# Moving four additions of a Strassen attention kernel from VectorE to accumulating DMAs issued by GpSimd

## The chip, the cores and the metric

The kernel runs on one core of one Trainium2 chip. The metric is the device time of one execution in microseconds (us). Two runs of the kernel before took 783.65 and 784.54 us, median 784.1.

The engines are named as in the profile: PE is TensorE's matmuls and PEld its weight loads, DVE is VectorE, ACT is ScalarE, POOL is GpSimd, SP is SyncE (it issues DMAs here). SBUF is the core's working memory; PSUM, in eight banks, is where matmuls leave their results.

## The reference

Plain attention over 8 batches, 2048 positions and a width of 512, in float32:

```python
scores = np.matmul(q, k.transpose(0, 2, 1)) / np.sqrt(d_k)
attn_weights = special.softmax(scores, axis=-1).astype(np.float32)
return np.matmul(attn_weights, v)
```

## The kernel before

The kernel works in float16 with float32 sums and cuts matmuls by Strassen's scheme in Winograd's form: a product of two-by-two blocks takes seven block products and some additions, in place of eight products. It does so for the scores (L271 to L326, class Group), for the weights times v (class Pair, from L474), and once more, a level deeper, for three of the seven products of that second stage (class Leaf). Softmax is computed without a maximum: ScalarE takes the exponential of the scores, and a column of ones beside v gives the row sums.

The work is cut in 32 periods, four to a batch; a period g covers 256 queries, in two blocks of 128, called a and b. Each period has an order written out by hand (SEQUENCES), a string of words; the periods 2 to 29 use four orders in turn, by the remainder of g by 4, and the first two and the last two have their own. Every engine and queue executes its instructions in the order in which the words put them, so the order of the words is the order of PE, DVE, ACT, POOL and SP, each for itself. A prime behind a word means that it belongs to the period before. The words that matter here:

- a dot: the next of 28 products of the scores of a period, two matmuls of 512 columns each (L299). L309 to L325 evacuate them: ScalarE copies, VectorE adds from PSUM (L319, L322), ScalarE takes exponentials (L239); e is one more exponential.
- a1, a5, a6, a7 and the same with b: a block's four products of the outer level, eight matmuls of 256 columns each (L512). Behind each stands a ScalarE copy of the result to the block's float32 rows in SBUF (L521, L524, L527, L530). Rows are cut in four quarters of 256 columns: o2l, o1l, o1r, o2r. Product 5 goes to o2r, 6 to o1r, 7 to o2l, 1 to o1l.
- f and h, with a or b: the additions that the change touches (add_right). f does o1r = o1r + o2r, once products 5 and 6 have been copied; h does o2r = o2r + o2l, once product 7 has been copied. Since h writes what f reads, h comes after f.
- L1 to L7: the products of the leaf level, twelve matmuls of 128 columns each (L424), for both blocks at once: L1, L2, L6 and L3 give parts of block a, L5, L7 and L4 of block b. Each is followed by a VectorE addition to the rows (L431), which therefore has to find f and h done. They share one PSUM bank (L5 and L3 a second), so that a leaf product also waits for the addition of the one before.
- s0 to s3, xa0 to xb3, K, q, V, u, w, n: sums of weights, k, q and v on VectorE, f16 to f16.
- S0, S1: the scaled rows of a block (ScalarE, L444), and their stores, issued by SP (L447).
- lq, lk, lv: a load of a quarter of the next batch's q, k or v, 512 KB in f16, with a cast from float32, issued by POOL (L131, L211). tq, tk: its transpose by a DMA that SP issues (L155). q and k go through two staging buffers, so a load waits, on POOL, for the transpose that frees its buffer.

Of the kernel before, what the change touches and what calls it, by code (L numbers as in the profile page):

```python
# [12 lines left out]
def kernel(  # L13
# [21 lines left out]
    nc = tc.nc  # L35
# [24 lines left out]
    NP = B * NQT  # L60
# [117 lines left out]
    add, sub = nc.vector.tensor_add, nc.vector.tensor_sub  # L178
# [270 lines left out]
    def halves(g, m):  # L449

        o = rows[g % 2][:, m, 0:4 * H].rearrange("p (h d) -> p h d", h=4)
        return o[:, 1:3], o[:, 0:4:3]

    def out_rows(g, m, half):
        b, sp = divmod(g // 2, NSP)
        n = (2 * sp + half) * NT + g % 2 * 2 + m
        return out[b, n * P:(n + 1) * P].rearrange("p (h d) -> p h d", h=2)
# [13 lines left out]
    class Pair:  # L471
# [58 lines left out]
            nc.scalar.copy(out=self.o2l, in_=self.x[:, 0:H])  # L530

        def add_right(self, n):
            if self.leaf and n == 1:
                add(self.o1r, self.o1r, self.o2r)
            elif self.leaf:
                add(self.o2r, self.o2r, self.o2l)

        def scaled(self, out_, src, r):
            nc.scalar.activation(out=out_, in_=src, func=COPY, scale=r)
# [6 lines left out]
        def ready(self, half):  # L546

            self.parts[half] += 1
            if self.parts[half] == 2:
                nc.sync.dma_start(  # L550
                    out=out_rows(self.g, self.m, half), in_=halves(self.g, self.m)[half]
                )

# [51 lines left out]
    def pv(g, which):  # L605
# [3 lines left out]
        if (g, which[0]) not in pairs:  # L609
# [19 lines left out]
        ),  # L629
        'second': (  # L630
# [3 lines left out]
        ),  # L634
# [4 lines left out]
        ),  # L639
# [5 lines left out]
        ),  # L645
# [4 lines left out]
        ),  # L650
# [5 lines left out]
        ),  # L656
        'alone': (
            "s2' xa0' b7' xa2' xa1' fb' . L6' s4' lv1' e ya0 a1 hb' ya1 xb0 L5' . ya2 a5 xb1 L7' "
            "ya3 tk2' K20' xa3' a6 fa b5 xb2 K30' a7 xa0 q1' L4' L3' xb3 ha b1 s1 S0' L2 b6 xa2 "
            "S1' "  # L660
        ),
        'last': (
            "b1 s3' b7' xb0 xa1' L1' s2' a5 xa3' fb' s4' hb' a1 b5 L6' a3 L5' xb1 a6 L7' xb2 L3' "
            "xb3 a2 L4' S0' a7 S1' b3 b6 b2 b7 a4 b4 "
        ),
    }

# [224 lines left out]
```

## Time and profile before

One execution was profiled. All times of instructions come from it.

| | |
|---|---|
| median of two runs | 784.1 us |
| the profiled execution | 782.76 us |
| its span, first to last instruction | 780.9 us |
| PE busy | 775.5 us |
| DVE busy | 742.4 us |
| ACT busy | 630.8 us |
| POOL busy | 72.2 us |
| granted TensorE clock | 1.00 |
| HBM read, written | 100.70 MB, 33.55 MB |

A line of the profile's groups gives the line in the kernel, the engine, the operation, the tile written and those read, the shape, and the count; behind the bar the busy time of all, the mean of one in ns, and the engine's idle time in front of them. Matmuls are pipelined, so their recorded durations overlap; the step from one start to the next tells the pace. A line of the waits gives the total, the number of waits and the longest one. In the timeline a line begins with start and length.

### The profile page before, as it was taken

Reading aid. Unit: us, or ns where it says so; the run is one execution under the profiler, and the core shown is the slowest. Engines: PE = TensorE matmul, PEld = TensorE weight load, DVE = VectorE, ACT = ScalarE, POOL = GpSimd, SP = SyncE. Lnnn points to the kernel's source line nnn. Section 1 sums busy time; section 2 is a strip of 40 time slices with the busy share of each in tenths; the row PEclk is TensorE's granted clock in tenths of the full one; section 3 lists DMA queues with packets and bytes.
Section 4 is the critical chain, followed back from the end, with each engine's and each line's share of the span. In section 5 each row is a group of like instructions: output and inputs, shape, how many; then the busy total and the mean of one; then the engine's idle time right before and its main releaser. Section 6 shows DMA issues by size and latency. Waiting matters only on the chain.

```text
span 780.9 us, 17260 instructions
## 1 busy us (share of the span) xinstructions
PE 775.5 (99%) x6681; PEld 538.5 (69%) x6681; DVE 742.4 (95%) x1460; ACT 630.8 (81%) x1146; POOL 72.2 (9%) x106
## 2 busy tenths in 40 slices
PE   9999999999999999999999999999999999999997
PEld 6566766667666776667666676766766667766687
DVE  5799999999999999999999999999999999999996
ACT  5887788887888878888788887888788887888863
POOL 4011100011000110001100100001000010000000
PEclk9999999999999999999999999999999999999999
DMA  9999776889859999578895879859788797930024
GB/s 226 182 170 153 160 169 134 157 158 169 181 100 148 197 155 187 111 153 179 111 205 118 175 152 149 188 116 167 164 151 174 135 152 156 168 95 29 28 72 146
DMA packets 196386, 115.97 MB, mean 149 GB/s; under 512 B 122448, under 2 KB 187088, under 8 KB 196304
## 3 DMA queue, kind: packets, MB, share of 16 engines
q0 software_dynamic: 49664, 49.29, 43.0%
q1 hardware_dynamic: 146352, 65.26, 34.0%
q8 instruction: 52, 0.85, 0.4%
q10 hardware_dynamic: 288, 0.33, 0.1%
q14 instruction: 30, 0.25, 0.1%
HBM read 100.70 MB, written 33.55 MB: 172 GB/s over the span
## 4 chain that ended last, share of the span: by engine, by line
PE 99%; DMA 1%; SPq 0%; ACT 0%; DVE 0%; issue 0%
PE t L299 48%; PE t L512 29%; PE t L424 19%; PE t L244 1%; PE t L259 1%; PE t L165 1%; DMA rows<-in_k_dram 1%; PE t L597 0%; SPq L141 0%; ACT stage L813 0%; SPq L760 0%; DVE rows L542 0%; PE t L790 0%
## 5 line engine op out<-in xcount | busy, mean ns | idle before, releaser
L299 PE MATMUL t<-qraw,kraw 128*128 128x512 f16 x732 | 192.2, 379 | 0.0
L512 PEld LDWEIGHTS <-s 128*128 128x128 f16 x1536 | 150.1, 98 | 50.4 <-issue 0.2
L424 PEld LDWEIGHTS <-right 128*128 128x128 f16 x2232 | 140.1, 97 | 38.3
L299 PEld LDWEIGHTS <-kraw 128*128 128x128 f16 x984 | 93.1, 98 | 77.1
L299 PE MATMUL t<-qs,ks 128*128 128x512 f16 x492 | 139.9, 379 | 0.0
L512 PE MATMUL t<-vt,s 128*128 128x257 f16 (+1 forms) x1024 | 131.8, 273 | 0.0
L239 ACT ACTIVATE right<-cz 128x1024 f16<-128x1024 f32 x123 | 130.2, 1058 | 1.3 <-DVE cz L319 0.8
L431 DVE TENSOR_TENSOR rows<-t,rows 128x384 f32<-128x384 f32 x217 | 119.7, 552 | 7.9 <-PE t L424 4.4
L313 ACT COPY cz<-t 128x512 f32<-128x512 f32 x122 | 71.5, 586 | 33.9 <-PE t L299 31.7
L299 PEld LDWEIGHTS <-ks 128*128 128x128 f16 x738 | 67.5, 98 | 39.9 <-issue 0.3
L239 ACT ACTIVATE right<-t 128x512 f16<-128x512 f32 x138 | 83.2, 606 | 12.5 <-PE t L299 3.8
L319 DVE TENSOR_TENSOR cz<-t,cz 128x512 f32<-128x512 f32 x123 | 84.3, 685 | 6.0 <-PE t L299 6.0
L239 ACT ACTIVATE left<-t 128x512 f16<-128x512 f32 x128 | 76.6, 599 | 16.3 <-PE t L299 13.4
L322 DVE TENSOR_TENSOR cz<-t,cz 128x512 f32<-128x512 f32 x123 | 84.3, 685 | 3.2 <-PE t L299 2.9
L316 ACT COPY cz<-t 128x512 f32<-128x512 f32 x123 | 72.9, 592 | 13.7 <-PE t L299 11.4
L444 ACT ACTIVATE rows<-rows,scales 128x512 f32<-128x512 f32 x124 | 82.8, 722 | 0.1
L424 PE MATMUL t<-vh,right 128*128 128x128 f16 (+1 forms) x1004 | 76.4, 218 | 0.0
L309 ACT COPY t<-t 128x512 f32<-128x512 f32 x121 | 70.2, 580 | 4.8
L299 PE MATMUL t<-qs,kraw 128*128 128x512 f16 x246 | 73.2, 379 | 0.0
L299 PE MATMUL t<-qraw,ks 128*128 128x512 f16 x246 | 73.1, 379 | 0.0
L512 PE MATMUL t<-vh,left 128*128 128x256 f16 x512 | 66.7, 273 | 0.0
L512 PE MATMUL t<-vh,s 128*128 128x256 f16 x512 | 66.4, 273 | 0.0
(93 smaller groups left out, 997.3 us busy)
## 6 DMA issues: line engine op xcount, KB each, us to landing
out_dram<-rows SPq DMA_DIRECT2D x127, 256.0 KB, 2.8
vh<-in_v_dram POOLq DMA_DIRECT2D x32, 512.0 KB, 9.6
stage<-in_q_dram POOLq DMA_DIRECT2D x28, 512.0 KB, 6.0
stage<-in_k_dram POOLq DMA_DIRECT2D x28, 512.0 KB, 6.8
right<-in_k_dram POOLq DMA_DIRECT2D x2, 512.0 KB, 12.9
rows<-in_q_dram SPq DMA_DIRECT2D x2, 256.0 KB, 3.6
cz<-in_q_dram SPq DMA_DIRECT2D x2, 256.0 KB, 4.4
cz<-in_k_dram SPq DMA_DIRECT2D x2, 256.0 KB, 4.5
```

The costliest lines, as they stand in the source:

```text
L165: nc.tensor.transpose(tr[:, m, dc, :], src[:, n + m, dc * P:(dc + 1) * P], ident)
L239: nc.scalar.activation(out=out_, in_=in_, func=EXP, scale=inv_sqrt_d)
L299: nc.tensor.matmul(dst[:], lhs[:, j, dc, :], rhs[:, :, dc, :], start=(n in (1, 5) and dc == 0), stop=(dc == 1), skip_group_check=True,)
L309: self.edges[0](out=self.y[:], in_=self.x[:])
L313: self.edges[1](out=self.cz[:, 0, :], in_=self.z[:])
L316: nc.scalar.copy(out=self.cz[:, 1, :], in_=self.x[:])
L319: nc.vector.tensor_add(self.cz[:, 0, :], self.x[:], self.cz[:, 0, :])
L322: nc.vector.tensor_add(self.cz[:, 1, :], self.z[:], self.cz[:, 1, :])
L424: nc.tensor.matmul(to[:, h * Q:h * Q + w], lhs[:, j, h, :], rhs[:, j, 0:w], start=(n in (1, 2, 5) and h == 0 and j == 0), stop=(j == NK - ...
L431: nc.vector.tensor_add(o, part, o)
L444: nc.scalar.activation(out=o, in_=o, func=COPY, scale=scales[:, g % 2, m, 1 - h:2 - h])
L512: nc.tensor.matmul(dst[:, 0:width], lhs(j), rhs(j), start=(first and j == 0), stop=(j == NJ - 1), skip_group_check=True,)
```

## The change

In the periods 1 to 29 the additions f and h of both blocks are made by DMAs that POOL issues, with the DMA adding its source to what stands at its destination. Period 0 and period 30 keep VectorE's additions (period 31 has none). All orders but the first are rewritten, with the same words except for their places. One store of the last block moves from SP's queue to ACT's. The diff, with the orders of the periods 1, 30 and 31 left out:

```diff
         def add_right(self, n):
-            if self.leaf and n == 1:
-                add(self.o1r, self.o1r, self.o2r)
-            elif self.leaf:
-                add(self.o2r, self.o2r, self.o2l)
+            if not self.leaf:
+                return
+            out, more = (self.o1r, self.o2r) if n == 1 else (self.o2r, self.o2l)
+            if 0 < self.g < NP - 2:
+                nc.gpsimd.dma_start(out=out, in_=more, accum_op=mybir.AluOpType.add)
+            else:
+                add(out, out, more)
...
             if self.parts[half] == 2:
-                nc.sync.dma_start(
+                last = self.which == "b" and self.g == NP - 1
+                (nc.scalar if last else nc.sync).dma_start(
                     out=out_rows(self.g, self.m, half), in_=halves(self.g, self.m)[half]
                 )
...
         1: (
-            "b7' e . w0' fb' w1' . L2' a1 w3' hb' . a5 s3' . . e . a6 w2' xa2' . . xa3' u3' . "
-            "L1' s2' . fa L5' tq1' . . . . L6' e . s4' n3' a7 ha . xb2 . tk1 lk3 xb0 xb1 L7' . . "
-            ". . e L3' xb3 . L4' . . . lk2 b1 s1 S1' L2 q0 q2 . s3 S0' . L1 . b6 e K00 b5 "
+            "e u2' xb0 xa0' . . a1 . . e V31' w1' n0' xa1' n1' xa3' . . . n3' a5 L2' . . . s3' "
+            "tq1' . hb' L1' s2' . . e xb1 a6 fa w3' . u3' . n2' L6' w2' . . s4' tk1 a7 lk3 e . "
+            "xb2 L5' L7' xb3 . . . . L3' . K00 . q0 ha q2 . L4' lk2 S0' b1 s1 s3 S1' b5 b6 . L2 "
+            ". . e L1 "
         ),
         2: (
-            "s2' b7' tk2' K20' . . xa0' . q1' fb' e L6' K30' ya0 hb' lv1' xa1' ya1 L5' K10' a1 "
-            "xa2' . . L7' . a5 ya2 . a6 q3 . . xb0 lq2 ya3 a7 s4' . xb1 xa3' xb2 . xa0 . b1 tk3 "
-            ". L3' . b5 . e xb3 . L4' s1 . b6 fa . xa1 S0' . e ha L2 . . b7 . fb . s3 hb L5 . . "
-            "lv3 . L1 S1' . K01 . lq3 "
+            "b7' fb' s2' K20' q1' tk2' . hb' . . e lv1' K30' L6' a1 xa0' xa1' ya0 K10' ya1 . . . "
+            "q3 L5' . a5 . xa2' . lq2 . a6 ya2 fa s4' . L7' e xb0 a7 . tk3 . L3' . L4' ya3 . S1' "
+            ". ha b1 . xb1 . . S0' xa0 e b6 xa3' xb2 xb3 . . . b5 xa1 . s1 s3 . b7 K01 . xa2 xa3 "
+            "K11 lv3 . fb . . lq3 "
         ),
         3: (
-            "e K21' . . a1 K11' a5 s2' . a6 xb0 lv2 . K31' L6' . e s4' . xa2' L7' . . fa tq3' . "
-            "xa3' L3' . xb2 tq2' . a7 . e L4' S1' . xb1 . . . xb3 e ha b1 s1 L2 . . s3 xa0 b5 . "
-            ". L1 s2 xa1 S0' . b6 fb . . . s4 xa2 b7 hb . q0 q1 . . . "
+            "a5 K21' a1 . . L2' a6 e . fa K31' hb' lv2 . L1' . a7 s2' . . . b1 s4' xb0 e tq3' . "
+            "ha L6' . xb1 tq2' . xb2 . xb3 s1 L5' . . . . e e L7' L3' s3 b6 . xa0 b5 . xa1 fb . "
+            "L4' S0' . . L2 . xa2 S1' . . L1 s2 s4 q0 . b7 . . . "
         ),
         0: (
-            "e L6' . V01 . L5' . V00 L7' . . q2' a1 e q3 . . ya2 ya0 . . lq0 e L3' . lk0 u0 V10 "
-            "tq0 V11 ya1 xb0 a5 . . . xa3' n0 a6 V20 . . V21 . . S0' b5 V30 u2 a7 xa0 . u1 n1 fa "
-            ". . lq1 ya3 b1 n2 . xb1 tk0 . xb2 . V31 L4' lv0 e . b6 . . xb3 s1 ha . lk1 . S1' "
-            "xa1 "
+            "q1' q2' . . e V00 a1 . V01 L6' V10 . . hb' . q3 L5' . . . e lq0 ya0 . lk0 L7' V30 "
+            "tq0 . L3' e . L4' a5 V20 S0' . V11 ya2 . . ya1 ya3 . . a6 fa S1' V21 . xb0 xa3' xb2 "
+            ". . lq1 a7 ha b5 . tk0 b1 . xb1 xb3 u0 e . u1 b6 fb lv0 . xa2 . . s1 . lk1 . w0 b7 "
         ),
```

More of the change, by code (lines that the diff above doesn't have):

```diff
@@ L630 @@
         'second': (
[3 rows of a table removed]
-        ),
[4 rows of a table removed]
-        ),
[5 rows of a table removed]
-        ),
[4 rows of a table removed]
-        ),
[5 rows of a table removed]
[3 rows of a table added]
+        ),
[5 rows of a table added]
+        ),
[5 rows of a table added]
+        ),
[4 rows of a table added]
+        ),
[4 rows of a table added]
         ),
         'alone': (
-            "s2' xa0' b7' xa2' xa1' fb' . L6' s4' lv1' e ya0 a1 hb' ya1 xb0 L5' . ya2 a5 xb1 L7' "
-            "ya3 tk2' K20' xa3' a6 fa b5 xb2 K30' a7 xa0 q1' L4' L3' xb3 ha b1 s1 S0' L2 b6 xa2 "
-            "S1' "
+            ". b7' xa0' s2' K20' xa1' e ya0 q1' xa2' lv1' . ya1 xb0 a1 L6' fb' ya2 a5 xb1 s4' "
+            "ya3 a6 b5 xa3' K30' fa xb2 a7 hb' L5' ha b1 tk2' xa0 L7' L3' b6 xb3 S0' L4' xa1 fb "
+            "b7 xa2 S1' L2 "
         ),
         'last': (
-            "b1 s3' b7' xb0 xa1' L1' s2' a5 xa3' fb' s4' hb' a1 b5 L6' a3 L5' xb1 a6 L7' xb2 L3' "
-            "xb3 a2 L4' S0' a7 S1' b3 b6 b2 b7 a4 b4 "
+            "a5 s1' xb0 a1 s3' xa3' L1' s2' hb' b1 xb1 b5 L5' a3 L6' s4' a6 xb2 a2 L7' xb3 L3' "
+            "S0' a7 L4' b3 b6 S1' b2 b7 a4 b4 "
         ),
```

6 rows, old and new, of the table SEQUENCES are left out of this document.

## The prediction

> **What bounds the kernel now.** The page's first part says which engines are full, and its fourth which of them the end waits for.
>
> ```profile
> span 780.9 us, 17260 instructions
> PE 775.5 (99%) x6681; PEld 538.5 (69%) x6681; DVE 742.4 (95%) x1460; ACT 630.8 (81%) x1146; POOL 72.2 (9%) x106
> PE 99%; DMA 1%; SPq 0%; ACT 0%; DVE 0%; issue 0%
> ```
>
> VectorE is 95% busy and is what the change relieves, but the chain of waits goes through TensorE for 99% of the span. Two things can hide in such a 99%: TensorE may wait in short pieces, and the modelled ends of its matmuls may cover gaps. The view of waits settles the first, and the view by stretches says where idle time is at all (columns: stretch, length, then busy time and instructions of each engine, granted clock, DMA share, GB/s).
>
> ```profile
> PE t L790 <- DVE vt L747: 1.2, 1, 1.2
> PE t L165 <- ACT stage L813: 0.3, 1, 0.3
> ```
>
> ```profile
> 0.00:20.00 20.00, 18.50 (x170) 13.25 (x171) 11.12 (x25) 10.30 (x17) 9.66 (x21) 1.00 1.05 226
> 20.00:100.00 80.00, 80.00 (x623) 51.76 (x622) 74.53 (x155) 64.33 (x116) 9.10 (x13) 1.00 1.01 167
> 100.00:700.00 600.00, 600.00 (x5148) 414.42 (x5146) 583.96 (x1131) 500.61 (x912) 53.43 (x72) 1.00 0.81 155
> 700.00:760.00 60.00, 60.00 (x550) 43.57 (x549) 58.79 (x122) 46.99 (x87) 0.00 (x0) 1.00 0.10 36
> 760.00:781.00 21.00, 16.98 (x199) 15.51 (x196) 13.99 (x33) 8.54 (x18) 0.00 (x0) 1.00 0.43 151
> ```
>
> TensorE's two waits are both in the opening, which the change doesn't touch. From 20 to 760 us it is never idle, at the full granted clock. For the second question I take the step from one start to the next in the timeline, which no modelled end can blur, and the counts of the three matmul lines from 100 to 700 us (L299, L512 and L424 in this order).
>
> ```profile
> 412.52 0.59 PE L299 MATMUL t<-qs,ks 128*128 128x512 f16 x2
> 412.95 1.04 PE L512 MATMUL t<-vh,s 128*128 128x256 f16 x8
> 413.83 0.59 PE L299 MATMUL t<-qs,ks 128*128 128x512 f16 x2
> 415.56 0.83 PE L424 MATMUL t<-vu,right 128*128 128x128 f16 x12
> 416.23 1.03 PE L299 MATMUL t<-qraw,kraw 128*128 128x512 f16 x4
> ```
>
> ```profile
> 100.00:700.00 600.00, 357.75 (x1416) 1.00 0.81 155
> 100.00:700.00 600.00, 204.61 (x1608) 1.00 0.81 155
> 100.00:700.00 600.00, 146.69 (x2124) 1.00 0.81 155
> ```
>
> Two matmuls of 512 columns take 412.95 - 412.52 = 0.43 us, eight of 256 take 413.83 - 412.95 = 0.88, and twelve of 128 take 416.23 - 415.56 = 0.67. Packed at that pace the counts need 1416 x 0.2165 + 1608 x 0.1094 + 2124 x 0.0558 = 306.6 + 175.9 + 118.5 = 601 us, in a stretch of 600. So TensorE streams without gaps, and VectorE, though nearly full, is never late. That is the main fact: the change removes no matmul, so outside the two ends it has nothing to win.
>
> **The change part by part.** *The additions that go.* The rows of L534 and L536, and the timeline around one of them:
>
> ```profile
> L536 DVE TENSOR_TENSOR rows<-rows 128x256 f32<-128x256 f32 x62 | 26.0, 419 | 0.0
> L534 DVE TENSOR_TENSOR rows<-rows 128x256 f32<-128x256 f32 x62 | 25.9, 418 | 0.0
> ```
>
> ```profile
> 400.52 0.41 DVE L534 TENSOR_TENSOR rows<-rows 128x256 f32<-128x256 f32 x1
> 400.85 0.68 DVE L319 TENSOR_TENSOR cz<-t,cz 128x512 f32<-128x512 f32 x1
> ```
>
> 62 of each is two blocks in 31 periods; the periods 1 to 29 give 4 x 29 = 116 of the 124. VectorE loses 116 x 0.419 = 48.6 us of records; by the steps, 0.33 us each, 38 us of its time, or 4 x 0.33 = 1.3 us in a period of about 23.8 us. On the path this is worth zero: the cover is TensorE's unbroken stream, and it stays. A bound from above on any gain is TensorE's whole idle time, 1.50 + 4.02 us in the first and last stretch, 0.7%.
>
> *The DMAs that come.* 116 issues on POOL, each 128 partitions x 1 KB. No row shows an accumulating DMA or one from SBUF to SBUF. The nearest (KB each, then the median us from issue to landing), with POOL's own issue time:
>
> ```profile
> out_dram<-rows SPq DMA_DIRECT2D x1, 128.0 KB, 1.9
> stage<-in_q_dram POOLq DMA_DIRECT2D x28, 512.0 KB, 6.0
> stage<-in_k_dram POOLq DMA_DIRECT2D x28, 512.0 KB, 6.8
> vh<-in_v_dram POOLq DMA_DIRECT2D x32, 512.0 KB, 9.6
> kraw<-stage SPq DMA_TRANSPOSE x28, 4.3
> ```
>
> ```profile
> L131 POOL DMA_DIRECT2D stage<-in_q_dram x28: 742/742/757, 36.9 to 669.3; - x28
> DMA to landing us min/median/max: 5.5/6.4/21.8
> ```
>
> The same bytes from the same tile land 1.9 us after an SP issue. A load through POOL, of four times the bytes, takes 6.0. The price, from issue to landing, lies between 1.9 and 6.0; I take 3.0, nearer to the row of equal size, with POOL's 0.74 us of issue and some 0.4 for the second read added to it. POOL's time is 116 x 0.74 = 86 us beside its 72: no bound. By the Trainium skill (DMA: Bandwidth & Descriptors, Anatomy of one DMA — SWDGE (gpsimd) path) a DMA of this path costs about 2.0 us plus its bytes at 436 GB/s; for 128 KB I estimate 2.3 us by it, the sum below would be the same, and no row here shows such a transfer alone.
>
> *What the price is worth.* The additions of one block are in series: hx rewrites what fx reads, so POOL issues hx only when fx has landed. Whoever comes late is the first leaf addition (L431) of that block, and behind it on VectorE, in order, the sums of scores (L319, L322) whose PSUM banks TensorE needs. So I walk the new orders with the steps above: 0.43 a dot, 0.87 an a or b product, 0.67 a leaf product, and the copy that frees each addition:
>
> ```profile
> L530 ACT COPY rows<-t 128x256 f32<-128x256 f32 x62 | 23.1, 373 | 9.5 <-PE t L512 9.5
> ```
>
> The tightest place is order 2. The end of b6 lies in order 1, with ". L2 . . e L1" behind it (2.64 us); in order 2, b7' ends at 0.87 and L5' at 0.87 + 3 x 0.43 + 0.67 + 0.87 + 3 x 0.43 + 0.67 = 5.68. So from b6 to the end of L5' there are 8.32 us. fb can start 0.37 after b6, hb not before b7's copy at 2.64 + 0.87 + 0.37 = 3.88. At 3.0 us each, fb lands at 3.4 and hb at 6.9: 1.4 us to spare. VectorE begins to wait once twice the price plus 0.37 passes 8.32, at 3.97 us. The next is order 0: b7 ends 1.30 before the end of order 3, and L5' ends 4.81 into order 0, so after the copy hb has 6.11 - 0.37 = 5.74 us. The hb' that order 1 issues stands on POOL behind two loads of order 0, lv0 and lk1: lk1 waits for tk0 (word at 16.8, plus 4.3 of landing, 21.1), is issued by 21.9 and lands some 7 to 10 us later, 28.7 to 31.5; the period ends at 22.5, so hb lands by about 10 of order 1, and L5' ends there at 14.0. The a blocks have more: L2 ends 9 us or more after the copy that frees ha, with one load at most between. So at 3.0 us no leaf addition waits, and the term is zero; at 4.5 it would be 7 x 1.05 us of VectorE's waiting, which the 1.3 us freed in each period absorb.
>
> *The loads behind them on POOL.* POOL now does a queue of its own waits:
>
> ```profile
> POOL stage L131 <- DMA qraw<-stage: 250.9, 24, 20.9
> POOL stage L131 <- DMA kraw<-stage: 177.4, 22, 21.3
> ```
>
> Until now it stood waiting for a transpose and issued the load at once. In order 0, lq0 and lk0 now stand behind hb', which is issued about when the period begins; 6.0 to 6.8 us later they land, before tq0's word at 7.2. If they come late, SP stands at tq0, with the stores of S0' (10.3) and tk0 (16.8) behind it, and the first sum that needs q is q0 late in order 1, over 25 us on. Zero, and the cover is that distance.
>
> *DMA traffic.* The row of POOL's queue:
>
> ```profile
> q0 software_dynamic: 49664, 49.29, 43.0%
> ```
>
> 116 x 128 = 14848 packets more, at 43.0% / 49664 each, are 13% of the engines' span, twice that if a read-modify-write costs double. The steady stretch has a share of 0.81 and the opening ran at 1.01 to 1.05 with more GB/s, so there is room: zero.
>
> *The new orders and the last store.* The words of TensorE are the same in number, so their worth is zero while nothing waits. The last b store moves from SP's queue to ACT's, beside another store of the tail; in the last stretch that can save or cost one issue, under 0.4 us.
>
> Sum against the profiled execution: 780.9 span + 0, and 1.9 around it, 782.8. The median of the runs shown is 1.3 above that execution, so I forecast 784.1.
>
> **The rivals.** *Slow additions* (slower). If an accumulating DMA costs what a q load costs, 6.0 us, then in order 2 hb lands at 0.37 + 12.0 = 12.37 against 8.32: VectorE stands 4.05 us, in each of the 7 periods with this order, and 0.26 in the 7 of order 0. The freed 1.3 us absorbs part, so TensorE loses 2.7 to 4.3 us seven times, 19 to 30: about 808. It passes 2% (15.7 us, 2.2 a place) at a price of 5.1 to 5.8 us. For it speaks that every POOL row is at 5.5 or more; against it that those move four times the bytes, from HBM.
>
> *Behind the loads* (slower). Additions share POOL's DMA queue with loads. If a load took the longest landing of the row above, 21.8, in order 0, hb would land at 21.9 + 21.8 - 22.5 = 21.2 of order 1, 7.2 after L5' ends; seven times, 50 us: 834. That longest one is from the opening's rush, so I give it little.
>
> *Descriptors held by VectorE.* If POOL could only issue in VectorE's pauses, each DMA would be later by up to one VectorE instruction, 0.7 us in the rows above: 3.7 each, still under 3.97, and 784 to 786. Against it: 28 issues took 742 to 757 ns while VectorE was 97% busy. The Trainium skill (SBUF — State Buffer, SBUF: two separate sides) warns of this starvation, for VectorE's two-port modes; the issue times here don't show it.
>
> *VectorE sets the pace after all* (faster). Then its 38 us would come back, 746. TensorE's packed steps exclude it; only the ends, at most 5.5 us, could shrink: 778.6.
>
> **How the numbers follow.** Zero sum, a price up to about 5 us: 0.79, with its own range from 783 to 790. Slow additions: 0.15. Behind the loads: 0.03. Held descriptors: 0.02, within 2%. Faster at the ends: 0.01, and faster by over 2% is excluded but for an error of mine: 0.01 for the class. So within 2% (about what a measurement of this kernel can tell from no change) 0.81, slower 0.18. The range goes from 782.0, the ends a little shorter, to 798.0, which takes in prices up to some 5 us; what is left out above is about 0.17.
>
> **What would show it.** Right: the accumulating DMAs land in a median near 3 us; VectorE's busy time falls to about 694 us (8 additions stay); TensorE is still never idle from 20 to 760 us; waits of L431 for such a DMA are rare and under 1 us. Wrong: landings of 4 us or more, L431 or L319 waiting for rows<-rows in order 2, with TensorE idle just behind it; POOL's loads later and SP standing at a transpose while K sums on VectorE wait.

## The result and the profile after

The changed kernel takes 818.4 us (median of two runs, 816.4 and 820.4) against 784.1: a ratio of 1.045, interval 1.043 to 1.047, so 34 us slower, above the top of my range at 798.0. The profiled execution took 816.36 us around a span of 814.4. Where the runs of a kernel below spread by more than 1.5%, the text compares those within 1.5% of its fastest.

The page's parts 1 and 4 of the changed kernel, to be read beside those of before:

```profile
span 814.4 us, 17487 instructions
PE 783.9 (96%) x6681; PEld 540.2 (66%) x6681; DVE 712.9 (88%) x1344; ACT 626.7 (77%) x1146; POOL 175.0 (21%) x222
PE 71%; DMA 18%; issue 4%; DVE 3%; ACT 2%; POOL 1%; SPq 0%; POOLq 0%; DVEq 0%; ACTq 0%
```

VectorE is lighter, as meant, and now also idle: it is busy for 88% of a longer span, where it was 95%. The chain of waits, which was TensorE for 99%, goes through DMAs for 18%. The view by stretches, for the same 600 us as before:

```profile
100.00:700.00 600.00, 576.93 (x4883) 395.25 (x4882) 530.57 (x981) 469.48 (x860) 138.79 (x168) 0.99 1.05 169
```

Before, this stretch held 5148 matmuls without a pause. Now it holds 4883, and TensorE is idle for 600 - 576.93 = 23 us of it. The 265 missing matmuls are 265 / 5148 x 600 = 31 us of work: most of the 34 us. Idle time accounts for 23 of the 31; PE's busy time for the same 6681 matmuls grew by 8 us as well, from 775.5 to 783.9 (the last section has a reason for part of that). The DMA share went from 0.81 to 1.05. The groups and DMA rows (KB each, us from issue to landing) that answer to those of the prediction:

```profile
L537 POOL DMA_DIRECT2D rows<-rows x116 | 101.1, 880 | 481.5 <-ACT rows L527 169.2 <-ACT rows L530 64.6 <-DVE s L352 46.7
```

```profile
L539 DVE TENSOR_TENSOR rows<-rows 128x256 f32<-128x256 f32 x8 | 3.3, 415 | 0.0
```

```profile
rows<-rows POOLq DMA_DIRECT2D x116, 128.0 KB, 4.9
stage<-in_q_dram POOLq DMA_DIRECT2D x28, 512.0 KB, 8.9
stage<-in_k_dram POOLq DMA_DIRECT2D x28, 512.0 KB, 7.4
qraw<-stage SPq DMA_TRANSPOSE x28, 8.3
kraw<-stage SPq DMA_TRANSPOSE x28, 7.8
```

```profile
DMA to landing us min/median/max: 2.6/4.9/16.6
```

The last fence is the landing row of L537 alone: an addition lands in 2.6 us at best, 4.9 in the median, 16.6 at worst. The transposes, which the change moves but doesn't alter, went from 4.3 to 7.8 us (k) and from 4.4 to 8.3 (q). Of the waits of the changed kernel, these five, longest first, show who stands for something late (POOL's are left out, and so are those that wait for TensorE or follow from the ones shown):

```profile
DVE ks L185 <- DMA kraw<-stage: 16.5, 7, 4.2
PE t L424 <- DVE rows L431: 16.3, 14, 3.2
ACT rows L524 <- DMA out_dram<-rows: 14.1, 5, 4.5
DVE rows L431 <- DMA rows<-rows: 8.1, 5, 2.4
PE t L512 <- ACT rows L521: 5.6, 3, 2.6
```

Before, the list had one of the five, and it was short:

```profile
ACT rows L524 <- DMA out_dram<-rows: 2.5, 2, 1.9
```

Three kinds of place lie behind these rows. In order 1, K00 (L185) waits on VectorE for the late transpose tk1, with leaf additions queued behind it and TensorE behind those. At the start of order 3, ScalarE's copy of product a5 (L524) waits for the store of the same rows, and the next product waits for the copies. Only the third kind, L431 waiting for an addition, is the one I had priced, and it is the smallest: 8.1 us of VectorE, and 3.2 us more at 596 us, which the view puts down to TensorE although the addition in front landed just then, at 596.3.

Why tk1 is late can be followed on the queues of SP and POOL in the second batch. The timeline of before on SP (start, length; a line of L155 is a transpose):

```profile
130.18 1.61 SPq L155 DMA_TRANSPOSE qraw<-stage  x1
145.45 1.88 SPq L155 DMA_TRANSPOSE kraw<-stage  x1
154.25 3.39 SPq L155 DMA_TRANSPOSE qraw<-stage  x1
157.75 1.78 SPq L155 DMA_TRANSPOSE kraw<-stage  x1
```

These are tq0, tk0, tq1 and tk1. The same four after, and what POOL did ahead of them:

```profile
138.78 2.40 SPq L155 DMA_TRANSPOSE qraw<-stage  x1
148.32 7.23 SPq L155 DMA_TRANSPOSE kraw<-stage  x1
156.18 5.71 SPq L155 DMA_TRANSPOSE qraw<-stage  x1
168.37 1.33 SPq L155 DMA_TRANSPOSE kraw<-stage  x1
```

```profile
132.02 0.85 POOL L537 DMA_DIRECT2D rows<-rows  x1 [6.56 <-ACT rows L530]
132.56 1.10 POOL L131 DMA_DIRECT2D stage<-in_q_dram  x1
133.32 1.12 POOL L131 DMA_DIRECT2D stage<-in_k_dram  x1
146.72 0.90 POOL L537 DMA_DIRECT2D rows<-rows  x1 [12.28 <-ACT rows L527]
147.66 0.76 POOL L131 DMA_DIRECT2D stage<-in_q_dram  x1
161.96 0.78 POOL L131 DMA_DIRECT2D stage<-in_k_dram  x1 [7.41 <-issue]
```

The line at 132.02 is hb: POOL stood 6.6 us for ScalarE's copy, and lq0 and lk0 went out behind it, at 132.6 and 133.3. Then POOL stood 12.3 us at fa, with lq1 behind it. So tk0 (148.32) runs beside lq1, takes 7.2 us to issue where it took 1.9, and lands after 12.6 us where it took 3.9. The load lk1 needs the buffer that tk0 frees and goes out at 162.0 (the last line), and tk1, which needs lk1, starts at 168.4 in place of 157.8. What tk1 itself cost, from issue to landing, before and after:

```profile
DMA to landing us min/median/max: 3.8/3.8/3.8
```

```profile
DMA to landing us min/median/max: 9.4/9.4/9.4
```

### The profile page after: what moved, and what is told of

Same layout as the page of the kernel before. It is cut to its first block, busy times and chain, and to the rows that moved or that the text cites. A ratio compares the mean times of both kernels' runs of the same rounds, so it can differ in the third digit from the quotient of the medians.

```text
span 814.4 us, 17487 instructions
## 1 busy us (share of the span) xinstructions
PE 783.9 (96%) x6681; PEld 540.2 (66%) x6681; DVE 712.9 (88%) x1344; ACT 626.7 (77%) x1146; POOL 175.0 (21%) x222
## 4 chain that ended last, share of the span: by engine, by line
PE 71%; DMA 18%; issue 4%; DVE 3%; ACT 2%; POOL 1%; SPq 0%; POOLq 0%; DVEq 0%; ACTq 0%
PE t L299 34%; PE t L512 20%; PE t L424 13%; DMA rows<-rows 10%; DMA kraw<-stage 4%; DMA out_dram<-rows 3%; PE t L244 1%; DVE rows L431 1%; PE t L259 1%; ACT rows L444 1%; PE t L165 1%; POOL stage L131 1%; DMA rows<-in_q_dram 1%; DVE qs L202 1%; DVE qraw L204 0%
## 5 line engine op out<-in xcount | busy, mean ns | idle before, releaser
L537 POOL DMA_DIRECT2D rows<-rows x116 | 101.1, 880 | 481.5 <-ACT rows L527 169.2
L431 DVE TENSOR_TENSOR rows<-t,rows 128x384 f32<-128x384 f32 x217 | 119.0, 552 | 38.7 <-PE t L424 26.1
L512 PE MATMUL t<-vt,s 128*128 128x256 f16 (+1 forms) x1024 | 132.8, 275 | 5.6 <-ACT rows L521 5.6
L299 PEld LDWEIGHTS <-ks 128*128 128x128 f16 x738 | 70.2, 98 | 52.3 <-issue 2.1
L239 ACT ACTIVATE right<-t 128x512 f16<-128x512 f32 x138 | 83.7, 609 | 12.3 <-PE t L299 6.8
## 6 DMA issues: line engine op xcount, KB each, us to landing
right<-in_k_dram POOLq DMA_DIRECT2D x2, 512.0 KB, 12.6
```

Source lines behind the costliest of these rows:

```text
L239: nc.scalar.activation(out=out_, in_=in_, func=EXP, scale=inv_sqrt_d)
L299: nc.tensor.matmul(dst[:], lhs[:, j, dc, :], rhs[:, :, dc, :], start=(n in (1, 5) and dc == 0), stop=(dc == 1), skip_group_check=True,)
L431: nc.vector.tensor_add(o, part, o)
L512: nc.tensor.matmul(dst[:, 0:width], lhs(j), rhs(j), start=(first and j == 0), stop=(j == NJ - 1), skip_group_check=True,)
L537: nc.gpsimd.dma_start(out=out, in_=more, accum_op=mybir.AluOpType.add)
```

## The experiments

I set four theories against each other: late loads (A), late additions (B), the added bytes (C), the new orders by themselves (D). Medians and ratios are against the kernel before, run on the same chip.

**What VectorE's time is worth.** The kernel before, with

```diff
         def add_right(self, n):
+            if 0 < self.g < NP - 2:
+                return
```

> The kernel before, with the additions f and h of the periods 1 to 29 left out altogether: VectorE has 38 to 49 us less to do and nothing comes in its place. If TensorE's packed stream is the bound, as I read it, the time stays within 0.2% of before, 782.5 to 784.5. If VectorE holds the kernel after all, it falls to 745 to 775.

Measured (e5): 783.2 us, ratio 0.9999 (0.9989 to 1.0008). Taking the additions away for nothing gains nothing. In these orders the change could not win, whatever carries the additions. This is shown, and it was the main reading of the prediction.

**The orders alone.** The changed kernel with VectorE's additions, then without any:

```diff
-            if 0 < self.g < NP - 2:
-                nc.gpsimd.dma_start(out=out, in_=more, accum_op=mybir.AluOpType.add)
-            else:
-                add(out, out, more)
+            add(out, out, more)
```

> The changed kernel's orders, with all additions on VectorE again. Four theories stand. A, late loads: the accumulating DMAs stand ahead of loads on POOL, the loads go out later and run beside transposes, both become slow, and sums and copies wait for them. B, late additions: leaf additions on VectorE wait for accumulating DMAs that land late behind loads. C, traffic: the added bytes slow all DMAs in proportion. D, orders: the new orders lose the time whoever adds. A, B and C expect 783 to 788 us here, with transposes landing in about 4.4 us as before; D expects 810 to 820.

Measured (e1): 804.3 us, 1.027 (1.021 to 1.033), k's transposes at 5.5 us. None of the four theories had this number: A, B and C stood for no loss and D for nearly all of it. The new orders lose 21 us by themselves. Whether by VectorE's load or by places, the next one asks (its edit: `if not 0 < self.g < NP - 2: add(out, out, more)`, and nothing else).

> The changed kernel's orders, with the additions of the periods 1 to 29 left out: VectorE is as light as in the changed kernel, and no DMA is added. It splits the 21 us that the new orders cost with VectorE's additions. If VectorE's load did it, 783 to 786. If the new places of stores, copies and transposes collide by themselves, 790 to 800, with ACT's copies of L524 waiting for stores.

Measured (e6): 799.8 us, 1.021 (1.019 to 1.023). VectorE is light here and no DMA is added, yet 16.6 us are lost, and this is where TensorE and ScalarE stood:

```profile
ACT rows L524 <- DMA out_dram<-rows: 23.7, 6, 5.1
PE t L512 <- ACT rows L521: 12.0, 5, 3.2
```

In order 2 the store S0 went from the slot at 18.1 us of the period to 16.8, but behind S1 on SP, while a5, whose copy overwrites the stored rows, went from 1.7 us of order 3 to its very start. So I swapped the two stores, first here and then in the changed kernel:

```diff
-            "q3 L5' . a5 . xa2' . lq2 . a6 ya2 fa s4' . L7' e xb0 a7 . tk3 . L3' . L4' ya3 . S1' "
-            ". ha b1 . xb1 . . S0' xa0 e b6 xa3' xb2 xb3 . . . b5 xa1 . s1 s3 . b7 K01 . xa2 xa3 "
+            "q3 L5' . a5 . xa2' . lq2 . a6 ya2 fa s4' . L7' e xb0 a7 . tk3 . L3' . L4' ya3 . S0' "
+            ". ha b1 . xb1 . . S1' xa0 e b6 xa3' xb2 xb3 . . . b5 xa1 . s1 s3 . b7 K01 . xa2 xa3 "
```

> The new orders with the additions of the periods 1 to 29 left out, and the two stores of order 2 swapped. Without the swap this lost 16.6 us, and each of its stalls over 1 us was ACT's copy L524 waiting for a store. If that place is all that is wrong with the new orders by themselves, 783 to 786. If the swap only moves the collision, 790 to 800.

Measured (e13): 784.4 us, 1.002 (1.001 to 1.003). One swap of two words gives back 799.8 - 784.4 = 15.4 us. With the additions left out, the new orders lose at this place and nearly nowhere else.

> The changed kernel, with two words swapped in order 2: S0, the store of block a, goes out at S1's place, and S1 at S0's. ACT's copies into the same rows at the start of order 3 (L524) then find the store landed; three to four stalls of 0.6 to 2.8 us, with the slow clock behind two of them some 8 to 12 us, go: 805 to 811. If these stalls have another cause, 814 to 820.

Measured (e8): 814.4 us, 1.040 (1.038 to 1.042), 4 us better than the changed kernel and short of what I expected. ScalarE's waits for stores fell from 14.1 to 3.9 us, but VectorE's for tk1 rose:

```profile
DVE ks L185 <- DMA kraw<-stage: 21.0, 6, 4.7
PE t L424 <- DVE rows L431: 21.5, 11, 3.6
```

So the losses don't add up. As I read it, a period that stands at one place gives the next DMA time to land; no run separates that.

**Late loads or late additions.** K00 moved from the middle of order 1 to its end, where the orders of before have it:

```diff
-            "xb2 L5' L7' xb3 . . . . L3' . K00 . q0 ha q2 . L4' lk2 S0' b1 s1 s3 S1' b5 b6 . L2 "
-            ". . e L1 "
+            "xb2 L5' L7' xb3 . . . . L3' . . q0 ha q2 . L4' lk2 S0' b1 s1 s3 S1' b5 b6 . L2 "
+            ". . e K00 L1 "
```

> The changed kernel, with one word moved: K00, the first sum of the next batch's k, goes from the middle to the end of order 1, as in the orders of before. Theory A says that VectorE stood there for the late transpose tk1 (L185, seven places), and TensorE behind it: six stalls of order 1, some 16 to 20 us, go, so 796 to 802. If the additions' own landings (B) or the added bytes (C) cost the time, it stays at 814 to 820.

Measured (e7): 816.8 us, 1.043 (1.041 to 1.045). The waits of L185 for the transpose are gone from the list, and the time is not. In their place:

```profile
PE t L512 <- DVE s L354: 13.3, 6, 3.0
DVE rows L431 <- issue: 12.2, 3, 4.3
DVE rows L431 <- DMA rows<-rows: 9.9, 6, 2.9
```

L431 now waits for its additions directly: ha in order 1, which was late as well, ha in order 3, and hb in order 2. By its time the run stands with B and C and against A, but its waits show that both are there: the late transpose had hidden late additions. Then the opposite, all load words moved forward, so that POOL issues them as soon as a transpose frees their buffer (lv1 behind lk2, lv3 behind lq2, lq3 and lv2 ahead of fb, the next period's lq0 and lk0 into order 3, lq1 and lv0 ahead of fa; `^` behind a word is the next period's):

```diff
-            "q3 L5' . a5 . xa2' . lq2 . a6 ya2 fa s4' . L7' e xb0 a7 . tk3 . L3' . L4' ya3 . S1' "
+            "q3 L5' . a5 . xa2' . lq2 lv3 . a6 ya2 fa s4' . L7' e xb0 a7 . tk3 . L3' . L4' ya3 . S1' "
...
-            "K11 lv3 . fb . . lq3 "
+            "K11 lq3 lv2 . fb . . "
...
+            "ha L6' . xb1 tq2' . xb2 . xb3 s1 lq0^ lk0^ L5' . . . . e e L7' L3' s3 b6 . xa0 b5 . xa1 fb . "
...
+            "tq0 lq1 lv0 . L3' e . L4' a5 V20 S0' . V11 ya2 . . ya1 ya3 . . a6 fa S1' V21 . xb0 xa3' xb2 "
```

> The changed kernel, with the load words moved in front of additions that become ready later, so that POOL issues each load soon after the transpose that frees its buffer, as before. The additions stay accumulating DMAs. A expects transposes to land in 4 to 5 us again and 784 to 795 us. B expects no gain or a loss, 815 to 840, since more additions now stand behind loads. C and D expect about 818.

Measured (e4): 815.5 and 828.2 us. The k transposes land in 5.3 us again, so A is right about them, but the time is no better than the changed kernel's 816.4 to 820.4, as B has it. In order 2, fb now stood behind lk2 and lv1 and landed 12.0 us after its issue, hb could only go out behind it, and VectorE stood in front of L431 meanwhile (columns: start, length; idle time in brackets):

```profile
281.60 0.68 DVE L205 TENSOR_TENSOR qs<-qraw,qs 128x1024 f16<-128x1024 f16 x1
288.89 0.56 DVE L431 TENSOR_TENSOR rows<-t,rows 128x384 f32<-128x384 f32 x1 [6.62 <-issue]
```

The old orders, with f and h right in front of their leaf products, show what late additions do without distance (the changed kernel with SEQUENCES of before; one line of many):

```diff
-            "q3 L5' . a5 . xa2' . lq2 . a6 ya2 fa s4' . L7' e xb0 a7 . tk3 . L3' . L4' ya3 . S1' "
+            "xa2' . . L7' . a5 ya2 . a6 q3 . . xb0 lq2 ya3 a7 s4' . xb1 xa3' xb2 . xa0 . b1 tk3 "
```

> The orders of before, with the accumulating DMAs. In these orders f and h stand close in front of their leaf products. B expects the worst here, 840 us or more, with L431 waiting long for rows<-rows. A expects over 800, by late loads and slow transposes, as after or worse. C expects about 818, as the bytes are the same. D expects 784 to 790.

Measured (e2): 872.5 us, 1.114 (1.103 to 1.125). The new orders do keep the additions early; that is what they are for.

Two tries to place everything well, with full additions. In the first, the stores are swapped, lq2 is behind fa, lv1 and lv3 behind ha, lq3 behind fb, lv2 behind ha, and lq0, lk0, lq1 and lv0 stand as in e4:

```diff
-            "q3 L5' . a5 . xa2' . lq2 . a6 ya2 fa s4' . L7' e xb0 a7 . tk3 . L3' . L4' ya3 . S1' "
+            "q3 L5' . a5 . xa2' . . a6 ya2 fa lq2 s4' . L7' e xb0 a7 . tk3 . L3' . L4' ya3 . S0' "
...
+            ". ha lv1' lv3 b1 . xb1 . . S1' xa0 e b6 xa3' xb2 xb3 . . . b5 xa1 . s1 s3 . b7 K01 . xa2 xa3 "
+            "K11 . fb lq3 . . "
...
+            "ha lv2 L6' . xb1 tq2' . xb2 . xb3 s1 lq0^ lk0^ L5' . . . . e e L7' L3' s3 b6 . xa0 b5 . xa1 fb . "
```

> The changed kernel with its DMA additions and bytes, and only places moved: in order 2 the stores swapped as before, lq2 behind fa (so that tk3 runs without it), lv1 and lv3 behind ha, lq3 behind fb; in order 3 lv2 behind ha and the next period's lq0 and lk0 brought forward; in order 0 lq1 and lv0 in front of fa. If the 34 us are all waits by place (late loads in order 1, a late store in order 3, late additions), and the additions as such cost nothing, 784 to 792. If the added bytes or the additions' own length cost time wherever they stand, 805 or more.

Measured (e10): 814.0 and 824.4 us, the other four runs from 830.6 to 851.4. In the second, lk0 goes behind fb:

```diff
-            "ha lv2 L6' . xb1 tq2' . xb2 . xb3 s1 lq0^ lk0^ L5' . . . . e e L7' L3' s3 b6 . xa0 b5 . xa1 fb . "
+            "ha lv2 L6' . xb1 tq2' . xb2 . xb3 s1 lq0^ L5' . . . . e e L7' L3' s3 b6 . xa0 b5 . xa1 fb lk0^ . "
```

> The kernel of the run before with one more word moved: lk0 goes behind fb in order 3. There fb stood on POOL behind lk0, which waited for a late tq2, and hb behind it came 3 to 6 us after the leaf addition of L5 that needs it (TensorE's stalls at 432.9 and 538.4 us of that profile). If all that is left is waits by place, 784 to 800, and no stall before L5 in order 0. If additions through the loads' queue are always late somewhere, because DMAs stretch beside each other, it stays over 805.

Measured (e12): 803.9 us in the fastest run, between the two answers that I had set against each other, and 824.7 to 833.7 in the other three. The profile of e10, taken in its fastest run, shows what is left. Around 212 us the transpose tq2 and the v load lv2 started together and landed in 8.7 and 9.1 us. Around 408 us the same pair took twice that (the first two lines, tq2 and lv2), and behind it TensorE stood 5.9 us:

```profile
DMA to landing us min/median/max: 17.1/17.1/17.1
DMA to landing us min/median/max: 17.8/17.8/17.8
439.17 0.58 PE L424 MATMUL t<-vt,right 128*128 128x128 f16 x4 [5.94 <-DVE rows L434]
```

Between the two, lk0 waited for tq2 until 425.9, fb stood behind lk0 and took 8.4 us, and hb, which the leaf addition of L5 needs, could only go out at 435.6. Two such pairs stand in this profile, at 408 and 514 us, each with a stall of 5.9 us some 25 us later; that the wide spread of the runs comes of their number is likely and not shown. e12 takes lk0 out of this chain; none of the places tried took the whole loss away.

**Bytes.** The additions cut to a quarter of their columns, first in the changed kernel, then in the places of e12:

```diff
-                nc.gpsimd.dma_start(out=out, in_=more, accum_op=mybir.AluOpType.add)
+                nc.gpsimd.dma_start(out=out[:, 0:64], in_=more[:, 0:64], accum_op=mybir.AluOpType.add)
```

> The changed kernel, with each accumulating DMA adding 64 of its 256 columns; the other three quarters of these additions are left out. The queue on POOL and its waits stay, a quarter of the added bytes stays. C expects the loss of 34 us to fall to a quarter, 790 to 795. A and B expect most of it to stay, 805 to 818, since place and waits are the same. D expects 818.

Measured (e3): 802.4 us, 1.025 (1.021 to 1.028): 16 of the 34 us go with three quarters of the bytes, and the rest stays. All of TensorE's stalls of 1 us and more in the periods are in order 1 now. No theory had this number.

> The places of the run e12, with accumulating DMAs of a quarter of the columns (the rest of these additions is left out). If the added bytes in the DMA queues are what remains in e12, 784 to 795. If it is the landing behind loads in POOL's DMA queue, whatever the size, 800 to 830 as there.

Measured (e15): 784.2 us, 1.002 (1.001 to 1.004). The stretch of 100 to 700 us:

```profile
100.00:700.00 600.00, 598.10 (x5127) 412.65 (x5126) 556.60 (x1025) 494.20 (x905) 144.37 (x175) 1.00 0.93 160
```

With the places of e12 and a quarter of the bytes, TensorE streams again but for 1.9 us, although every issue, wait and queue on POOL is still there. So what e12 has left, 20 us in its fastest run, comes with the bytes of the additions. e3 and e15 have the same DMAs in different places, and so measure the places: 802.4 - 784.2 = 18.2 us.

Last, e12 with full additions and without the loads of v of the batches from the third on:

```diff
-            load_v(b, c)
+            if b < 2:
+                load_v(b, c)
```

> The places of the run e12, with its full accumulating DMAs, and the loads of v left out from the third batch on (old v is used again): 24 loads of 512 KB fewer beside the transposes. If the remaining loss comes of transposes and additions that stretch beside those loads, stalls stay in the first two batches and nearly none come behind them, 784 to 795. If the additions' own bytes and length are enough, 800 to 830.

Measured (e16): eight runs from 784.7 to 797.8 us, ratio 1.015 (1.012 to 1.017). Of the 21 us that e12 loses in its fastest run, about half remain in the middle of these runs, and nearly none in the run of 784.7. So full additions can run at almost no loss, and the loads beside them have a part in it. The run doesn't tell whether those loads cost by their bytes or by standing ahead of additions in POOL's queue, and the 784.7 is the run that was profiled, so that no trace shows where the others lose.

**GpSimd in place of its DMAs.** The same additions as instructions of GpSimd, in the places of the change and then in those of e12:

```diff
-                nc.gpsimd.dma_start(out=out, in_=more, accum_op=mybir.AluOpType.add)
+                nc.gpsimd.tensor_add(out, out, more)
```

> The changed kernel with the additions computed by GpSimd itself in place of its DMAs: the same places and waits on POOL, no added DMA traffic, and an addition is done when the instruction ends, not when a DMA lands. Late additions go; the late loads of order 1 and the store of order 3 stay if they come from the places: 800 to 812. If the DMAs' landings or bytes made all the loss, 784 to 790. If GpSimd's reads of SBUF hold VectorE up, VectorE's additions show longer durations than before and it is slower than 812.

Measured (e11): 799.1 us, 1.020 (1.018 to 1.022), just under the first answer, with k's transposes at 8.2 us and all stalls of 1 us and more in order 1: late loads behind POOL's waits, with no addition's DMA in any queue.

> The places of the run e12 (loads early, stores swapped), with the additions computed by GpSimd itself: no DMA is added and an addition ends with its instruction. With the changed kernel's places the same additions took 799. If the late loads behind POOL's waits were those 16 us, 783 to 788. If additions on POOL cost time wherever they stand, 795 or more.

Measured (e14): 794.2 us, 1.014 (1.012 to 1.016). The late loads are gone, no stall in the periods is over 1 us, and still 11 us are lost. VectorE itself is slower, which the third answer of e11 had allowed for and which e11 shows too (mean ns of one, behind the comma; the third line is the changed kernel's):

```profile
L352 DVE TENSOR_TENSOR s<-right 128x1024 f16<-128x1024 f16 x48 | 40.6, 856 | 0.0
L396 DVE TENSOR_TENSOR left<-right 128x1536 f16<-128x1536 f16 x31 | 33.2, 1070 | 0.2
L352 DVE TENSOR_TENSOR s<-right 128x1024 f16<-128x1024 f16 x48 | 32.2, 683 | 0.0
```

Of the additions of L352 in this shape that e14's timeline lists one by one, the 17 with no addition of GpSimd beside them took 0.68 or 0.69 us, and of the 15 with one, 14 took 0.75 or 1.22. By the Trainium skill (SBUF — State Buffer, Who interferes with whom) a VectorE instruction with two inputs in SBUF and a GpSimd instruction that reads SBUF keep each other waiting at a shared read port; these rows agree. With DMAs in place of GpSimd's instructions VectorE is not held: 683 ns against 684 before. That all 11 us come of it is not shown.

## Why the prediction was wrong, point by point

*TensorE is the bound and VectorE's time is worth nothing.* Right, and shown by e5. VectorE's busy time fell to 712.9 us and not to the 694 that I had named as a sign: records overlap, so that 48.6 us of them are not 48.6 us of busy time. In e5, with the same instructions gone, it is 707.6.

*The additions' price, 3.0 us from 1.9 to 6.0.* Near for the best case, 2.6 (no run measures the 0.4 that I had put in it for the second read), and wrong as a price in this kernel: the median is 4.9 and one in the profile 16.6. I had walked the orders with one number for all, and reckoned with late loads ahead of an addition only in order 0. Even the a blocks, which I had called safe, came late: in the order 3 that begins at 108 us, fa landed 7.9 us and ha 8.7 us after its issue, 15 us after the copy that frees ha, and TensorE stood 0.9 us for the leaf addition behind.

*Traffic, zero, since the opening ran at a share of over 1.* This step failed. I had taken the opening's share of 1.05 for room. A share in that view is time that packets took, not room that is left: around the slowest DMAs of the changed kernel (a transpose issued at 188.1 us that took 18.8, an addition issued at 193.4 that took 16.6) it went up while the rate fell.

```profile
197.00:199.00 2.00, 2.00 (x19) 1.39 (x16) 1.63 (x5) 1.44 (x4) 0.00 (x0) 1.00 1.62 54
205.00:207.00 2.00, 2.00 (x13) 1.01 (x12) 1.52 (x2) 2.00 (x6) 0.00 (x0) 1.00 1.10 298
```

The last two columns: 54 GB/s at a share of 1.62, 298 at 1.10. I had reckoned with 13% more of the span; between 100 and 700 us the share rose by 0.24. Part of that is the other DMAs' packets, which now take longer. The queue whose 65 MB are those of the transposes and the stores shows it, before and after:

```profile
q1 hardware_dynamic: 146352, 65.26, 34.0%
q1 hardware_dynamic: 146208, 64.99, 40.5%
```

That is 0.340 x 780.9 = 266 us and 0.405 x 814.4 = 330 us for nearly the same packets. The share alone doesn't set how long a transpose takes: k's take 8.2 us in e11 at a share of 0.88 between 100 and 700 us, and 5.2 in e10 at 1.00, so it depends on what runs beside them. e3 against the changed kernel, and e15 against the fastest run of e12, measure the term: 16 and 20 us for three quarters of the bytes.

*The loads behind POOL's waits, zero, with 25 us of distance as cover.* This step failed too. I followed tq0 to the first sum of q and stopped there. The chain goes on, lq0, tq0, lq1 and lk0, tk0, lk1, tk1, because each load waits for the transpose in front of it, and at its end K00 stands on VectorE. Waiting sums of k were among my signs of being wrong, but I had put no price on them. e3 and e15 measure the term, the two stores included, at 18 us, with all of e3's stalls of 1 us and more in order 1. Without any addition's DMA the same step, from e11 to e14, is worth only 5 us, so that the late loads cost more where the additions' bytes are in the queues too.

*The new orders, zero while nothing waits.* This step failed: S0 behind S1, and a5 earlier, left a store too little time, and e6 less e13 is 15.4 us for that alone, with the additions left out. In the changed kernel the same swap gives 4 us (e8). I had walked the orders for f and h and not for the stores.

*The rivals.* "Slow additions" came nearest in time (808) but not in mechanism: the place it names, hb in order 2, stalled in e4 and e7, but only once in the profile of the changed kernel (TensorE stood 1.7 us until 597.6), whose largest wait is for a transpose. "Behind the loads" did happen in single cases, like the 16.6 us. Descriptors held by VectorE would have cost up to 0.7 us each; an addition's issue took 0.88 us in the mean where I had put 0.74, so if that played a part, it was a small one.

*What stays open.* Why a transpose and loads of POOL's queue that start together sometimes take 17 us and sometimes 9. The additions alone don't set it off: in e15, with a quarter of their bytes, tq2 and lv2 issued at 209.2 us took 17.2 and 13.1, in e13, without any addition, a transpose and a v load issued at 181.5 and 182.4 took 13.9 and 16.6, and before, a pair at 372 us took 13.1 and 12.0. So such pairs came before the change, and what the runs show is that they cost more with the full additions behind them; how much of that is their number and how much what stands behind them stays open. How the 34 us divide cannot be given as a sum, since the waits cover each other (e7, e8).

## What to carry to other kernels

Ask first whether the engine that is relieved is ever waited for; leaving its work out for one run answers it, as e5 did here. When a queue that was only waiting gets new work, follow every transfer behind it to the end of its chain, through the buffers, and treat each moved store like a moved load. DMAs off the critical path slowed those on it here (k's transposes from 4.3 to 7.8 us, additions from 2.6 to 16.6): price a new one beside its neighbours, not alone.

## What the runs showed of the hardware

Behind some stalls TensorE came back at half its clock. In the changed kernel this followed the stalls of 2.55, 2.41 and 2.59 us that ended at 212.7, 284.9 and 415.0 us. The first is followed by this stretch, with the granted clock third from the end:

```profile
213.00:216.00 3.00, 3.00 (x14) 1.56 (x12) 1.16 (x2) 1.83 (x4) 1.70 (x3) 0.51 1.01 116
```

So a stall can cost more than its length. By the Trainium skill (TensorE: Matmul & The Clock Gate, What's actually happening) the half clock comes after at least one idle window of about 3.4 us, and this window is free-running. The measurement differs in the length: these stalls were shorter than such a window. The stall of 3.2 us that ended at 180.4 us was followed by full clock, which a free-running window allows.
